# Attention on one core: the last ten pairs' queries and keys transposed by transfers inside SBUF

## The chip, the core and the metric

The kernel runs on one core of a Trainium2 chip. The metric is the device time of one execution in microseconds, lower is better; the inputs lie in HBM before, the output lies there after. The engines are PE (TensorE), DVE (VectorE), ACT (ScalarE), POOL (GpSimd) and SP (SyncE), which here only issues transfers. They run their own instruction streams in order and wait for each other through semaphores.

## What is computed

Softmax attention over 8 x 8 heads of 512 queries and 512 keys with 64 dimensions, in float32 at both ends:

```python
batch, heads, seq, dim = 8, 8, 512, 64
scale = 1.0 / np.sqrt(q.shape[-1])
scores = np.einsum('bhqd,bhkd->bhqk', q, k) * scale
attn = np.exp(scores - scores.max(axis=-1, keepdims=True))
attn = attn / attn.sum(axis=-1, keepdims=True)
return np.einsum('bhqk,bhkd->bhqd', attn, v)
```

## The kernel before

**Pairs and groups.** The 64 heads are taken two at a time: 32 pairs, numbered g from 0 to 31. Each head's 512 keys are four chunks c of 128. A block is one chunk of keys of one head against all 512 queries; a group is two blocks, in most pairs the same chunk of both heads. There are four groups a pair, 129 in all because the last is cut in two halves, and they are numbered m; group m belongs to pair m // 4 (the halves at the end aside).

**The way of one pair.** SP loads q, k and v of the pair, 256 KB each (L432; for v of pairs 20 to 24, `HALVED`, in two pieces, L430). POOL casts them to fp16: v into one of twelve tiles `vps` that hold a column of ones beside the 64 dimensions (L438), q and k into one tile `qkp` with both heads side by side (L448; five such tiles). PE transposes the eight 128x128 blocks of `qkp` into one PSUM tile (`transposes`, L472) and DVE copies that to SBUF as `tqk`, dimensions of both heads in the partitions (`copy`, L485; four such tiles). PE then makes the scores of a group: two matmuls of 64 x 512 that stand in the two halves of the array's rows (`scores`, L512), into one of three PSUM tiles `st`. ACT takes exp of the 128x1024 scores at once (L517) into one of 30 tiles `pt`. PE multiplies slices of 128 queries with the values (`values`, L619): a unit is one such slice of one head, four units a head, 65 columns each, the last the sum of the row. Seven units share a PSUM bank (two banks, which the transposes also use). DVE divides by the sum (`normalise`, L596 and L598) into a ring of 56 units in SBUF, and SP stores each head from there when its four units are done (L607, 128 KB).

**Groups on DVE.** For the groups in `ON_DVE` DVE replaces ACT's exp: `raise_` (L538) turns scores into the bits of a power of two and frees the `st` bank, and five passes (`pass_`, L552, L561, L571, L576 and L585) make from it two fp16 parts `pe` and `pd` whose sum is the exponential. The value matmuls of such a block run twice, once for each part.

**The order of the work.** Nothing is scheduled by a compiler: the order of each engine's stream comes from the class `Plan`, which steps through time with a duration for each kind of work and writes down what each engine takes next. `step_pe` prefers scores when a bank is free, then transposes of the next pair, then values. `step_dve` prefers copies that are needed soon, then raises, then normalises; passes go in where nothing else is due. `step_pool` and `step_dve` put out casts in the order of `self.due`, as soon as the load has landed and a `qkp` tile is free. A cast of pair g puts the load of pair g + 7 into SP's list (`emit`), since the float32 tile comes free with it (seven of each of q, k and v); `step_sp` works that list off in order, and normalises add stores to it. The first pair, its loads and the start are written out by hand (`first_pair`), and so are the last head's values (`last_values`, `finish`, L638 to L660). The plan only sets orders; on the chip each step still waits for its data.

Of the kernel before, what the change touches and what calls it, by code (L numbers as in the profile page):

```python
# [10 lines left out]
FP16 = mybir.dt.float16  # L11
U16 = mybir.dt.uint16
# [5 lines left out]
class Plan:  # L18
# [13 lines left out]
    STEP = 5  # L32
    CALM, KEEN = 9000, 4
    FIRST_UNIT = 4
    ON_DVE = (10, 16, 26, 34, 43, 52, 61, 68, 79, 82, 96, 105, 114)

    LATE_NORM, LATE_COPY, HURRY, SOON, BACKLOG = 1300, 1400, 900, 80, 1000
    SLACK, AHEAD = 0, 1
# [1 line left out]
    CAST, CAST_DONE, TO_POOL = 557, 130, 150  # L40
    FIRST_LAND, LOAD, STORE, LATENCY, ISSUE = 5200, 700, 350, 2300, 450
    RAW, QK16, NV = 7, 5, 12

    def __init__(self, groups, pairs, first):
        self.groups, self.pairs = groups, pairs
        self.pe, self.act, self.dve = 7000, self.FIRST_EXP, 6300
        self.pool, self.port, self.dma = 4600, 4600, self.FIRST_LAND
        self.m, self.tiled = first, True
        self.read = []
        self.exps = {}  # L50
        for m in range(first):
            self.act += self.EXP + self.EXP_FIXED
            self.exps[m] = self.act + self.EXP_DONE
            self.read.append(self.exps[m])
        self.tq = {0: 5800}
        self.transposed = {0: 5800}
        self.next_t = 1
        self.part_t = 0
        self.banks = [5100, 5800]
        self.todo = [(g, h) for g in range(pairs) for h in range(2)]  # L60
        self.last = self.todo.pop()
        self.last_part = 0
        self.head = None
        self.units = self.FIRST_UNIT
        self.member = {b: m for m, grp in enumerate(groups) for b in grp}
        self.ready = []
        self.passes = []
        self.passed = {}
        self.steps = []
        self.busy_dve = 0  # L70
        self.done_heads = 0

        late = {grp[0][0] for m, grp in enumerate(groups) if m in self.ON_DVE}
        due = []
        for g in range(pairs):
            scores = 5000 + 3380 * g
            if g:
                due += [(scores - 2300, g, "k"), (scores - 2290, g, "q")]
            due.append((scores + 4000 + (6000 if g in late else 0), g, "v"))
        self.due = sorted(due)  # L80
        self.uncast = list(self.due)
        self.casts = []
        self.landed, self.cast_done = {}, {}
        self.first_loads = [(g, n) for _, g, n in self.due if g < self.RAW]
        self.first_loads += [(self.RAW, "k"), (self.RAW, "q")]
        for x in self.first_loads:
            self.dma += self.LOAD
            self.landed[x] = self.dma
        self.loads = []
        self.sp = 1650 + 470 * len(self.first_loads)  # L90

    def note(self, t, *what):
# [2 lines left out]
    def emit(self, t, after):  # L95
        _, g, n = self.uncast.pop(0)
        shared = (g, n) == (1, "q")
        self.note(t, "cast", g, n, t > self.CALM)
        if not shared:
            self.casts.append((g, n, t if after is None else after + self.TO_POOL))  # L100
        if g + self.RAW < self.pairs:
            self.note(t, "load", g + self.RAW, n)
            self.loads.append(("load", g + self.RAW, n))
# [20 lines left out]
                self.cast_done[(g, n)] = t + self.CAST + self.CAST_DONE  # L124

    def step_sp(self, t):
        if not self.loads or self.sp > t:
            return
        what = self.loads[0]
        if what[0] == "load":  # L130
            _, g, n = what
            if g >= self.RAW and self.cast_done.get((g - self.RAW, n), 1e9) > t:
                return
            self.dma = max(self.dma, t + self.LATENCY - self.LOAD) + self.LOAD
            self.landed[(g, n)] = self.dma
        else:
            if what[1] > t:
                return
            self.dma = max(self.dma, t + self.LATENCY - self.STORE) + self.STORE
        self.loads.pop(0)  # L140
        self.sp = t + self.ISSUE
# [113 lines left out]
    def step_pe(self, t):  # L255
        if self.m == len(self.groups):
            self.values(t)
            return
        g = self.groups[self.m][0][0]
        backlog = self.act - t  # L260
        one, two = self.free() <= t, self.free(1) <= t
        if one and (two or backlog < self.HURRY or self.tiled):
            return self.scores(t)
        if not one and backlog < self.BACKLOG and self.free() < t + self.SOON:
            return
        if self.part_t:
            return self.transposes(t)
        if (
            self.next_t < self.pairs
            and self.next_t <= g + self.AHEAD  # L270
            and all(self.cast_done.get((self.next_t, n), 1e9) <= t for n in "kq")
            and self.bank(t) is not None
        ):
            return self.transposes(t)
        if not self.values(t) and one:
            self.scores(t)

    def step_dve(self, t):
# [8 lines left out]
        if now:  # L287
            g = self.groups[min(self.m + 1, len(self.groups) - 1)][0][0]
            job = min(now, key=lambda x: (x[1] != "copy" or x[2][0] > g, x[1] != "raise", x[0]))
            self.ready.remove(job)  # L290
            _, kind, what = job
# [8 lines left out]
            if kind == "norm":  # L300
                more = self.NORM_COLUMN * what[1]
                self.dve = t + self.NORM[0] + more
                self.banks[what[2]] = t + self.NORM[1] + more + self.TO_PE
                for _ in range((what[0] + what[1]) // 4 - what[0] // 4):
                    self.loads.append(("store", self.dve + 100))
            elif kind == "finish":
                self.dve = t + self.NORM[0] + 2 * self.NORM_COLUMN
            elif kind == "copy":
                held, done = self.COPY if what[0] != 1 else self.COPY_1
                self.dve = t + held  # L310
                self.banks[what[1]] = self.tq[what[0]] = t + done + self.TO_PE
            else:
                self.dve = t + self.RAISE[0]
                self.read[what[0]] = t + self.RAISE[1] + self.TO_PE
                self.passes += [(what[0], s) for s in range(len(self.PASSES))]
                self.passed = {(what[0], None): self.dve + self.PASS_DONE, **self.passed}
# [30 lines left out]
def kernel(  # L347
# [28 lines left out]
    cpool = ctx.enter_context(tc.tile_pool(name="const", bufs=1))  # L376
    lpool = ctx.enter_context(tc.tile_pool(name="load", bufs=7))
    qpool = ctx.enter_context(tc.tile_pool(name="qk16", bufs=5))
    tpool = ctx.enter_context(tc.tile_pool(name="tqk", bufs=4))
    ppool = ctx.enter_context(tc.tile_pool(name="pt", bufs=30))  # L380
    dpool = ctx.enter_context(tc.tile_pool(name="pd", bufs=4))
    wpool = ctx.enter_context(tc.tile_pool(name="work", bufs=2))
# [3 lines left out]

    NV = 12

    HALVED = range(20, 25)
    NU = 56  # L390
    ring = cpool.tile([P, NU, D], FP32, name="ring")
    vps = [cpool.tile([P, 2, NI, D + 1], FP16, name=f"vp{n}") for n in range(NV)]
# [14 lines left out]
    def source(src, g):  # L407
        b, h = g // ppb, 2 * (g % ppb)
        return src[b, h : h + 2].rearrange("h (p i) d -> p h i d", i=NI)
# [12 lines left out]
    def load(g, names):  # L422
        if g >= NP:
            return
        for name in names:
            src = {"q": q, "k": k, "v": v}[name]
            t = load_tile(g, name)
            if name == "v" and g in HALVED:
                for h in range(2):
                    nc.sync.dma_start(out=t[:, h], in_=source(src, g)[:, h])  # L430
                continue
            nc.sync.dma_start(out=t[:, :, :, :], in_=source(src, g))  # L432

    def cast(g, name):
# [29 lines left out]
    def transposes(g, n, bank):  # L464
        if n == 0:
            tqk[g] = tpool.tile([P, 2, S], FP16, tag="tqk", name=f"tqk_{g}")
        if n == 0 or g == 1:

            tps[g] = ps_x.tile([P, 2, NI, P], FP16, tag=f"x{bank ^ n}", name=f"tp_{g}_{n}")
        n = 1 - n  # L470
        for i in range(NI):
            nc.tensor.transpose(tps[g][:, n, i, :], qkp[g][:, n, i, :], ident)  # L472
        if g == 1 and n == 1:
            copy(g, n)

    def copy(g, n=0):
        if g == 1:
# [55 lines left out]

    def raise_(m):
        r = raised[m]
        r["u"] = wpool.tile([P, 2, S], U16, tag="u", name=f"u_{m}")
        dve(
            nc.vector.tensor_scalar(  # L538
                out=r["u"][:, :, :],
                in0=r["st"][:, :, :],  # L540
                scalar1=BITS,
                scalar2=BIAS,
                op0=AluOp.mult,
                op1=AluOp.add,
            )
        )
# [46 lines left out]
    def normalise(u, n):  # L593
# [8 lines left out]
                op=AluOp.mult,  # L602
            )
        )
        while heads and heads[0][2] + NI <= u + n:
            g, h, u0 = heads.pop(0)
            nc.sync.dma_start(  # L607
                out=source(out, g)[:, h], in_=ring[:, u0 % NU : u0 % NU + NI, :]
            )
# [152 lines left out]
    with tc.manual_schedule():  # L762
# [6 lines left out]
        for n in range(NV):  # L769
# [5 lines left out]
            "values": values,  # L775
            "load": load,
            "cast": cast_behind,
            "raise": raise_,
            "copy": lambda g, b: copy(g),
            "pass": pass_,  # L780
# [36 lines left out]
```

## Time and profile before

| | us |
|---|---|
| runs: 117.13, 117.09, 116.84; median | 117.09 |
| the profiled execution | 117.77 |
| its span, first to last instruction | 116.0 |
| DVE busy, with the four largest groups L598, L485, L538, L585 | 97.5: 22.6, 20.5, 15.8, 9.3 |
| POOL's casts of v, k, q | 20.2, 19.2, 18.4 |
| PE's scores, values from `pt`, transposes | 43.9, 45.2, 19.3 |
| SP's issues of 256 KB loads, from issue to landing | 5.0 to 5.3 |
| SP's issues of 128 KB stores, from issue to landing | 3.9 |

Busy times are of one execution with its own time, 117.77. An engine's mean time of one instruction counts from its start to its end; where the next one starts before that end, the two overlap, and the distance from start to start is what one of them really takes. HBM was read for 25.17 MB and written for 8.39 MB. The granted clock of TensorE was 0.999.

### The profile page before, as it was taken

Reading aid. Unit: us, or ns where it says so; the run is one execution under the profiler, and the core shown is the slowest. Engines: PE = TensorE matmul, PEld = TensorE weight load, DVE = VectorE, ACT = ScalarE, POOL = GpSimd, SP = SyncE. Lnnn points to the kernel's source line nnn. Section 1 sums busy time; section 2 is a strip of 40 time slices with the busy share of each in tenths; the row PEclk is TensorE's granted clock in tenths of the full one; section 3 lists DMA queues with packets and bytes.
Section 4 is the critical chain, followed back from the end, with each engine's and each line's share of the span. In section 5 each row is a group of like instructions: output and inputs, shape, how many; then the busy total and the mean of one; then the engine's idle time right before and its main releaser. Section 6 shows DMA issues by size and latency. Waiting matters only on the chain.

```text
span 116.0 us, 4294 instructions
## 1 busy us (share of the span) xinstructions
PE 105.4 (91%) x1663; PEld 69.5 (60%) x1663; DVE 97.5 (84%) x209; ACT 107.8 (93%) x120; POOL 57.6 (50%) x102
## 2 busy tenths in 40 slices
PE   7979988999999899999999999989999999999940
PEld 2545544665666557676655676558577667657630
DVE  1464599996999799999999999999999999996270
ACT  4499999999999999999999999999999999999930
POOL 2466836469464674753847568644634974000000
PEclk9999999999999999999999999999999999999999
DMA  3999999999999999999979999889998995821244
GB/s 95 323 328 374 384 378 383 384 380 374 381 333 330 309 362 324 305 318 356 369 248 291 319 317 295 266 264 338 346 310 267 361 309 171 266 94 50 91 138 138
DMA packets 35605, 33.84 MB, mean 292 GB/s; under 512 B 2688, under 2 KB 35584, under 8 KB 35584
## 3 DMA queue, kind: packets, MB, share of 16 engines
q1 hardware_dynamic: 35152, 33.24, 86.0%
q10 hardware_dynamic: 432, 0.33, 0.9%
q8 instruction: 13, 0.21, 0.8%
q14 instruction: 8, 0.07, 0.2%
HBM read 25.17 MB, written 8.39 MB: 289 GB/s over the span
## 4 chain that ended last, share of the span: by engine, by line
ACT 46%; PE 45%; issue 5%; DVE 2%; ACTq 0%
ACT pt L517 45%; PE st L512 17%; PE o L619 16%; PE tp L472 6%; PE st_0a L671 3%; ACT pt L721 1%; PE st L714 1%; PE tp_qb L709 0%; PE o_last L638 0%; DVE qt L751 0%; DVE ring L598 0%; PE tp_qa L709 0%; DVE obl L653 0%; PE st_0a L714 0%; DVE rc_last L652 0%
## 5 line engine op out<-in xcount | busy, mean ns | idle before, releaser
L517 ACT ACTIVATE pt<-st 128x1024 f16<-128x1024 f32 (+1 forms) x113 | 102.8, 1240 | 0.0
L512 PE MATMUL st<-tqk 64*128 64x512 f16 (+1 forms) x250 | 43.9, 380 | 4.0 <-ACT pt L517 2.7
L619 PE MATMUL o<-vp,pt 128*128 128x65 f16 x904 | 45.2, 195 | 0.5 <-POOL vp L438 0.2
L619 PEld LDWEIGHTS <-pt 128*128 128x128 f16 x904 | 38.5, 98 | 11.7 <-issue 8.7
L438 POOL CAST vp<-v 128x512 f16<-128x512 f32 x32 | 20.2, 631 | 13.4 <-DVE pd L585 5.0
L448 POOL CAST qkp<-q 128x512 f16<-128x512 f32 x30 | 18.4, 613 | 14.3 <-DVE pd L585 3.9
L448 POOL CAST qkp<-k 128x512 f16<-128x512 f32 x31 | 19.2, 619 | 9.2 <-PE st L512 2.2
L598 DVE TENSOR_TENSOR ring<-o,rc 128x448 f32<-128x448 f32 (+2 forms) x37 | 22.6, 612 | 1.3
L512 PEld LDWEIGHTS <-tqk 64*128 64x128 f16 x250 | 13.1, 93 | 16.7 <-issue 9.2
L485 DVE COPY tqk<-tp 128x1024 f16<-128x1024 f16 x30 | 20.5, 683 | 1.6 <-PE tp L472 1.4
L472 PE MATMUL tp<-ident,qkp 128*128 128x128 f16 x248 | 19.3, 220 | 0.4 <-DVE tqk L485 0.3
L472 PEld LDWEIGHTS <-qkp 128*128 128x128 f16 x248 | 14.1, 97 | 6.8 <-issue 3.9
L619 PE MATMUL o<-vp,pe 128*128 128x65 f16 x104 | 18.0, 195 | 0.2 <-DVE tqk L485 0.2
L619 PE MATMUL o<-vp,pd 128*128 128x65 f16 x104 | 17.9, 193 | 0.0
L538 DVE TENSOR_SCALAR u<-st 128x1024 uint16<-128x1024 f32 x13 | 15.8, 1217 | 1.6 <-PE st L512 1.5
L619 PEld LDWEIGHTS <-pe 128*128 128x128 f16 x104 | 10.2, 98 | 2.4 <-issue 2.4
L596 DVE RECIPROCAL rc<-o 128x7 f32<-128x7 f32 (+2 forms) x37 | 7.3, 196 | 5.0 <-PE o L619 4.6
L619 PEld LDWEIGHTS <-pd 128*128 128x128 f16 x104 | 10.2, 98 | 0.2 <-issue 0.2
L585 DVE TENSOR_TENSOR pd<-u,w 128x1024 f16<-128x1024 f16 x13 | 9.3, 714 | 0.2
L571 DVE TENSOR_TENSOR s<-m 128x1024 f16<-128x1024 f16 x13 | 8.8, 680 | 0.0
L552 DVE TENSOR_SCALAR m<-u 128x1024 uint16<-128x1024 uint16 x13 | 6.1, 470 | 0.1
L561 DVE TENSOR_SCALAR pe<-u 128x1024 uint16<-128x1024 uint16 x13 | 6.2, 476 | 0.0
(48 smaller groups left out, 32.3 us busy)
## 6 DMA issues: line engine op xcount, KB each, us to landing
out_dram<-ring SPq DMA_DIRECT2D x63, 128.0 KB, 3.9
k<-in_k_dram SPq DMA_DIRECT2D x31, 256.0 KB, 5.1
q<-in_q_dram SPq DMA_DIRECT2D x31, 256.0 KB, 5.3
v<-in_v_dram SPq DMA_DIRECT2D x27, 256.0 KB, 5.0
v<-in_v_dram SPq DMA_DIRECT2D x10, 128.0 KB, 4.0
k<-in_k_dram ACTq DMA_DIRECT2D x2, 128.0 KB, 2.9
q<-in_q_dram SPq DMA_DIRECT2D x2, 128.0 KB, 2.7
out_dram<-obl SPq DMA_DIRECT2D x1, 64.0 KB, 1.6
```

The source lines that it names most:

```text
L438: return nc.gpsimd.tensor_copy(out=vps[g % NV][:, :, :, 0:D], in_=raw[g]["v"][:, :, :, :])
L448: return nc.gpsimd.tensor_copy(out=dst, in_=src[:, :, :, :])
L472: nc.tensor.transpose(tps[g][:, n, i, :], qkp[g][:, n, i, :], ident)
L485: nc.vector.tensor_copy(out=tqk[g][:, :, :], in_=tps.pop(g).rearrange("p n i c -> p n (i c)"))
L512: nc.tensor.matmul(st[:, x, cols], kc, qc[:, cols], start=True, stop=True)
L517: nc.scalar.activation(out=pt[:, :, cols], in_=st[:, :, cols], func=EXP, scale=scale, bias=SHIFT)
L538: nc.vector.tensor_scalar(out=r["u"][:, :, :], in0=r["st"][:, :, :], scalar1=BITS, scalar2=BIAS, op0=AluOp.mult, op1=AluOp.add,)
L571: ins = nc.vector.tensor_tensor(out=r["s"][:, :, :], in0=mantissa, in1=mantissa, op=AluOp.mult)
L585: ins = nc.vector.tensor_tensor(out=r["rest"][:, :, :], in0=r["u"].bitcast(FP16)[:, :, :], in1=r["w"][:, :, :], op=AluOp.mult,)
L596: nc.vector.reciprocal(out=rc[:, 0:n], in_=o[:, x : x + n, D : D + 1])
L598: nc.vector.tensor_tensor(out=ring[:, u % NU : u % NU + n, :], in0=o[:, x : x + n, 0:D], in1=rc[:, 0:n].broadcast_to([P, n, D]), op=AluOp. ...
L619: nc.tensor.matmul(os[u // 7][:, u % 7, :], part[:, y * P : (y + 1) * P], vps[g % NV][:, h, c, :], start=(n == 0), stop=(n == len(parts) - 1),
```

## The change

Four things change.

- For the pairs from `TURNED` = 22 on, PE no longer transposes and DVE no longer copies. A transposing transfer that SP issues (`turn`) reads `qkp` and writes `tqk` in SBUF. The plan holds it back until the scores of pair g - 8 are made (eight `tqk` tiles now) and both casts are done, and counts 1500 ns of transfer time and 4000 ns to its landing. The casts of these pairs are due 9000 ns ahead of their scores in the plan, 2300 before.
- Two heads of a pair go out in one store where they follow each other and lie in the ring in one piece; heads at the end go out as before.
- The loads of v of pairs 20 to 24 are whole.
- Fourteen groups are on DVE, at other places; the tile `u` that `raise_` writes has four buffers, two before.

```diff
-    ON_DVE = (10, 16, 26, 34, 43, 52, 61, 68, 79, 82, 96, 105, 114)
+    ON_DVE = (8, 14, 23, 29, 41, 48, 58, 63, 69, 76, 87, 92, 107, 116)
...
+    TURNED, TQ = 22, 8
+    TURN, TURN_LATENCY, TURN_AHEAD = 1500, 4000, 9000
...
-                due += [(scores - 2300, g, "k"), (scores - 2290, g, "q")]
+                ahead = 2300 if g < self.TURNED else self.TURN_AHEAD
+                due += [(scores - ahead, g, "k"), (scores - ahead + 10, g, "q")]
...
+        if g >= self.TURNED and n == "q":
+            self.turns.append(g)
...
     def step_sp(self, t):
+        if self.turns:
+            g = self.turns[0]
+            if self.m > self.member[(g - self.TQ, 3, 1)]:
+                self.turns.pop(0)
+                self.note(t, "turn", g)
+                self.loads.append(("turn", g))
...
+        elif what[0] == "turn":
+            _, g = what
+            if max(self.cast_done.get((g, n), 1e9) for n in "kq") > t:
+                return
+            self.dma = max(self.dma, t + self.TURN_LATENCY - self.TURN) + self.TURN
+            self.tq[g] = self.transposed[g] = self.dma
...
-            self.next_t < self.pairs
+            self.next_t < self.TURNED
...
-                for _ in range((what[0] + what[1]) // 4 - what[0] // 4):
+                for _ in range((what[0] + what[1]) // 8 - what[0] // 8):
...
-    tpool = ctx.enter_context(tc.tile_pool(name="tqk", bufs=4))
+    tpool = ctx.enter_context(tc.tile_pool(name="tqk", bufs=Plan.TQ))
...
-    HALVED = range(20, 25)
...
-            if name == "v" and g in HALVED:
-                for h in range(2):
-                    nc.sync.dma_start(out=t[:, h], in_=source(src, g)[:, h])
-                continue
...
+    def turn(g):
+        tqk[g] = tpool.tile([P, 2, S], FP16, tag="tqk", name=f"tqk_{g}")
+        nc.sync.dma_start_transpose(
+            out=tqk[g].rearrange("p n (i c) -> p (n i) c", c=P),
+            in_=qkp[g].rearrange("p n i c -> p (n i c)"),
+        )
...
-        r["u"] = wpool.tile([P, 2, S], U16, tag="u", name=f"u_{m}")
+        r["u"] = wpool.tile([P, 2, S], U16, tag="u", name=f"u_{m}", bufs=4)
...
+        end = Plan.FIRST_UNIT + 4 * (2 * NP - 1)
         while heads and heads[0][2] + NI <= u + n:
-            g, h, u0 = heads.pop(0)
+            g, h, u0 = heads[0]
+            if h == 0 and u + n < end and u0 % NU + 2 * NI <= NU:
+                if len(heads) == 1:
+                    break
+                if heads[1] == (g, 1, u0 + NI):
+                    if u0 + 2 * NI > u + n:
+                        break
+                    del heads[:2]
+                    nc.sync.dma_start(
+                        out=source(out, g),
+                        in_=ring[:, u0 % NU : u0 % NU + 2 * NI, :].rearrange(
+                            "p (h i) d -> p h i d", h=2
+                        ),
+                    )
+                    continue
+            heads.pop(0)
             nc.sync.dma_start(
```

More of the change, by code (lines that the diff above doesn't have):

```diff
@@ L89, in __init__ @@
         self.loads = []
+        self.turns = []
+        self.stored = 0
         self.sp = 1650 + 470 * len(self.first_loads)
@@ L777 @@
             "cast": cast_behind,
+            "turn": turn,
             "raise": raise_,
```

## The prediction

> **What bounds the kernel now.** I read four views of the profile, in this order. First the page: busy shares, the chain and the costliest groups.
>
> ```profile
> span 116.0 us, 4294 instructions
> ...
> PE 105.4 (91%) x1663; PEld 69.5 (60%) x1663; DVE 97.5 (84%) x209; ACT 107.8 (93%) x120; POOL 57.6 (50%) x102
> ...
> q1 hardware_dynamic: 35152, 33.24, 86.0%
> ...
> ACT 46%; PE 45%; issue 5%; DVE 2%; ACTq 0%
> ...
> L517 ACT ACTIVATE pt<-st 128x1024 f16<-128x1024 f32 (+1 forms) x113 | 102.8, 1240 | 0.0
> ...
> L485 DVE COPY tqk<-tp 128x1024 f16<-128x1024 f16 x30 | 20.5, 683 | 1.6 <-PE tp L472 1.4
> L472 PE MATMUL tp<-ident,qkp 128*128 128x128 f16 x248 | 19.3, 220 | 0.4 <-DVE tqk L485 0.3
> ```
>
> By shares alone PE, DVE and ACT all look full, and the chain hands the time to ACT and PE about equally. The idle column decides: L517 never had its engine idle before it (0.0). Second, the timeline of ACT alone, which merges what runs without a gap:
>
> ```profile
> 7.53 1.02 ACT L721 ACTIVATE pt<-st 128x1024 f16<-128x1024 f32 x1 [0.28 <-PE st L714]
> 8.45 102.83 ACT L517 ACTIVATE pt<-st 128x1024 f16<-128x1024 f32 x113
> ```
>
> One unbroken stretch of 102.83 us: 111 full exponentials and two halves, so 102.83/112 = 0.918 us for each. The 1240 ns of the group row overlap; 0.918 is the price. The span is 8.45 us of start, this stretch to 111.28, and a tail of 4.7. PE's share of the chain is PE answering a bank that ACT has just released, inside ACT's queue. So only two things move the time: how many exponentials ACT makes, and whether one of them ever waits.
>
> Third, the same busy times by stage (columns: PE, PEld, DVE, ACT, POOL, clock, DMA share, GB/s):
>
> ```profile
> 60.00:70.00 10.00, 9.84 (x169) 6.73 (x169) 9.75 (x21) 10.00 (x12) 6.05 (x11) 1.00 0.94 299
> 70.00:80.00 10.00, 9.21 (x147) 5.88 (x147) 9.79 (x20) 10.00 (x12) 5.78 (x10) 1.00 0.89 282
> 80.00:90.00 10.00, 10.00 (x178) 6.99 (x175) 9.45 (x20) 10.00 (x13) 4.92 (x9) 1.00 0.97 313
> 90.00:100.00 10.00, 9.80 (x176) 6.80 (x173) 9.79 (x19) 10.00 (x12) 6.14 (x10) 1.00 0.83 278
> ```
>
> In the stretch where the new transfers run, 70 to 100 us, DMA already moves 282 to 313 GB/s. Fourth, DVE's timeline, where a start to the next start is what an operation really holds:
>
> ```profile
> 71.18 0.67 DVE L485 COPY tqk<-tp 128x1024 f16<-128x1024 f16 x1
> 71.78 1.21 DVE L538 TENSOR_SCALAR u<-st 128x1024 uint16<-128x1024 f32 x1
> 72.91 0.19 DVE L596 RECIPROCAL rc<-o 128x7 f32<-128x7 f32 x1
> 73.13 0.62 DVE L598 TENSOR_TENSOR ring<-o,rc 128x448 f32<-128x448 f32 x1
> 73.67 0.68 DVE L485 COPY tqk<-tp 128x1024 f16<-128x1024 f16 x1
> ```
>
> A copy holds 0.60, a raise 1.13, a normalise 0.76; the five passes, read the same way, 0.33, 0.33, 0.61, 0.46 and 0.61. A group on DVE holds 1.13 + 2.34 = 3.47 us.
>
> **The change, part by part.**
>
> *Fourteen groups on DVE for thirteen.* ACT makes 112 exponentials, not 113: one full one less, **-0.92 us**, on the path. DVE pays 3.47; PE pays 8 more value matmuls (104/13 = 8 a group), at some 0.034 apart 0.27 us, under ACT.
>
> *Ten pairs without transposes and copies.* PE loses 80 transposes; eight stand in the chain with 0.55, so 5.5 us. DVE loses 10 copies of 0.60, 6.0. Neither engine held ACT up in the stretch above, so this is worth nothing by itself; it pays for the 3.47 and 0.27. If the cover went (ACT no longer full), PE's 5.5 would count.
>
> *The new places.* Ten groups now stand at or before group 76, eight before. Scores of group 77 come when ACT has done 77-3-10 = 64 exponentials: 8.45 + 64 x 0.918 = 67.2 us. DVE, from its first copy at 8.1, has 59.1 us for 10 groups (34.7), 20 copies (12.0) and some 19 normalises (14.4): 61.1, 2.0 too much; with 8 groups it was 54.1 of 60.9. What is put off is passes (lowest in the planner's order; the u tiles go from two buffers to four, so several groups can wait). After that 44 us remain for 4 groups, 1 or 2 copies and 17 normalises, about 28. Bounds: 0 to +2.0 us; I take 0, since DVE was 98% busy from 60 to 80 before with ACT never idle. A late raise would hold one of the three score banks; the next-but-two scores wait behind it on PE, then ACT.
>
> *Ten transposing transfers on SP.* No row shows such a transfer. It moves 256 KB from SBUF to SBUF. Lower bound, as an ordinary load at the best rate in the page's slices (384 GB/s): 0.68 us of all 16 engines. Upper bound: a row of a transposed block is 128 fp16, 256 B, a quarter of the usual 1 KB packet; if each cost what a packet costs now (0.86 x 116.0 us x 16 / 35152 = 45 ns), 1024 of them take 2.9 us. From 70 to 100 us DMA moved (282 + 313 + 278) x 10 us = 8.73 MB, 22.7 us at 384 GB/s: 7.3 us are free. Ten turns need 6.8 at the lower bound, 29 at the upper. What doesn't fit eats lead. Pair 22's query cast (the 21st q row of L448) ended at 66.9; its first exponential, number 75 of L517's row, began near 8.45 + 75 x 0.918 = 77.3, now 0.9 sooner, and its scores must be begun some 0.9 (a slot of ACT, my estimate) before that: 75.5. So 8.6 us, less a landing of 5.1 to 5.3 like k and q loads: 3.4 of slack. The cast is due 6.7 us sooner (9000 for 2300), two pairs ahead in the order, and the five qkp buffers let it (its data landed long before): 10 us of slack. Cover: 7.3 + 10 = 17.3 us, or **1.73 us a turn**. Nearest row is the 256 KB load, so I take 0.68: cost 0 on the path; the upper bound costs 11.7 us.
>
> The Trainium skill, "DMA: Bandwidth & Descriptors", section Latency and other measured facts, gives a DMA transpose 261 GB/s where the middle dimension isn't contiguous and 350 to 400 where it is. By that page alone my estimate is 0.66 to 1.0 us a turn, inside the cover, and the sum would be the same with a smaller chance of late turns; no row of this trace shows such a transfer, so nothing here is built on it.
>
> *SP's queue.* A turn waits on SP for POOL's two casts and for PE's scores of pair g-8 (long done); behind it queue the loads and stores, and behind those POOL's casts and DVE's ring. SP already stands 8.2 us (17 times) on such casts without ACT noticing. Its issues fall: five v loads in one piece, -5; ring stores in twos where both heads lie in the 56-unit ring in one piece: pairs whose u0 % 56 is 52 (4 of 31) and the last stay single, so 63 becomes 36 if heads come in order; turns +10. Net -22 of about 0.43, so 9 us less on SP. A dispatch of a turn could take as long as the longest store's, 1.59 us: 10 x 1.2 more, near what was saved. Cost 0, bounds 0 and about +1 where a store blocks the ring. Same bytes, later by half a pair (1.7 us) against a ring seven pairs long: 0.
>
> *The tail.* After 111.28 come the last values, DVE's finish with a normalise between (0.55), and three stores; SP issued the last at 113.32, 0.8 us after its data (112.52), held up by a store that took 1.1 to issue. Fewer stores and a freer PE could take this out, or the normalise: -0.6 to +0.3. ACT's own last store at 112.96 stays, so I take -0.1.
>
> **Sum.** -0.92 + 0 + 0 + 0 - 0.1 = -1.0 us. The profiled execution took 117.77 (span 116.0 and 1.8 around it), giving 116.8; it was 0.68 above the median of the runs, 117.09, giving **116.1**, which I forecast.
>
> **Rivals.**
>
> *Turns land late* (slower). At 2.0 us a turn, ten need 20, 2.7 over the cover: PE stands at the first scores of a late pair, all PE work queues behind, ACT runs dry. 117.09 - 0.92 + 2.7 = 118.9. It decides from 1.73 us a turn. For it: DMA shares of 0.89 to 0.97, FIFO behind loads. Against: seven pairs of raw buffers, few loads left after 90 us. Chance 0.25.
>
> *VectorE becomes the bound before group 76* (no change). Half of the 2.0 lost as ACT waits after raises: 117.09 - 0.92 + 1.0 = 117.2. For: 61.1 in 59.1. Against: u's four buffers, DVE full before without harm. Chance 0.12.
>
> *Blocks one behind the other.* If each of a turn's eight 128x128 blocks took a latency of its own, as the smallest store here does (1.6 us), a turn would take 12.8 against 3.3 us a pair (102.83/31): 10 x 9.5 - 17 (the cover) = 78 us more, 117.09 - 0.92 + 78 = 194. Against: ordinary loads of 128 rows pay one latency. Chance 0.03. The Trainium skill, "VectorE: DVE Perf Modes", section The three transpose paths, gives 1309 ns for one 128x128 block by DMA against 390 on TensorE; eight in a row would be 10.5 us by that page. By that rule this change is a bad trade; no run here shows it yet.
>
> *Nothing else moves*: the forecast, 0.60.
>
> **Range and chances.** A measurement of this kernel can tell about 0.3% (0.35 us) from no change. Faster by more than that: 0.60, the forecast. Within it: 0.13 (DVE's bound, and mild lateness). Slower: 0.27 (late turns, one by one). The forecast's own range is 115.5 (the whole tail gain) to 116.6; the range, with the late turns up to 2.0 us, 115.5 to 118.9.
>
> **What would show it.** Right: L517 x112 in one stretch of about 101.9 us, idle 0.0; L485 x20; u x14; turns landing within 8 us of issue; ring stores near 36. Wrong: L517 with idle, released by PE whose scores waited for a DMA into tqk (late turns, after 75 us) or for u L538 (DVE, before 67 us); a DMA share at its ceiling from 70 to 100 us with POOL waiting for loads.

## The result: 121.46 us, 3.3% slower, and the profile after

The changed kernel takes 121.46 us (median of 120.67, 121.04, 121.87 and 123.31) against 117.11 before: ratio 1.0327, 95% interval 1.0266 to 1.0387. Executions fall into a faster and a slower state, and the ratio compares the faster ones (here without 123.31), so it is not the quotient of the two medians. The profiled execution took 121.87 with a span of 120.1, 4.1 more than before. On the page, the lines that answer to those shown of before:

```profile
span 120.1 us, 4117 instructions
...
PE 103.9 (87%) x1591; PEld 66.5 (55%) x1591; DVE 94.2 (78%) x205; ACT 107.6 (90%) x119; POOL 57.5 (48%) x102
...
PE 43%; ACT 22%; DVE 17%; DMA 10%; issue 5%; ACTq 0%
...
L538 ACT ACTIVATE pt<-st 128x1024 f16<-128x1024 f32 (+1 forms) x112 | 102.6, 1210 | 5.4 <-PE st L533 5.4
...
out_dram<-ring SPq DMA_DIRECT2D x25, 256.0 KB, 5.3
out_dram<-ring SPq DMA_DIRECT2D x13, 128.0 KB, 3.9
...
tqk<-qkp SPq DMA_TRANSPOSE x10, 4.8
```

The exponential is one less (x112), as meant; but ACT, which never stood, now stands 5.4 us, all of it released by PE's scores, and DMA has entered the chain with 10%. ACT's timeline says when:

```profile
8.43 71.60 ACT L538 ACTIVATE pt<-st 128x1024 f16<-128x1024 f32 x78
82.72 1.02 ACT L538 ACTIVATE pt<-st 128x1024 f16<-128x1024 f32 x1 [2.68 <-PE st L533]
83.92 1.02 ACT L538 ACTIVATE pt<-st 128x1024 f16<-128x1024 f32 x1 [0.18 <-PE st L533]
85.12 1.02 ACT L538 ACTIVATE pt<-st 128x1024 f16<-128x1024 f32 x1 [0.18 <-PE st L533]
87.47 1.02 ACT L538 ACTIVATE pt<-st 128x1024 f16<-128x1024 f32 x1 [1.32 <-PE st L533]
89.28 3.77 ACT L538 ACTIVATE pt<-st 128x1024 f16<-128x1024 f32 x4 [0.78 <-PE st L533]
93.35 23.09 ACT L538 ACTIVATE pt<-st 128x1024 f16<-128x1024 f32 x26 [0.30 <-PE st L533]
```

Up to 80.03 us the stretch is unbroken: nothing is lost in the two thirds with ten groups on DVE. Then six pauses, 5.44 us, and each restart costs 0.1 more (1.02 for an exponential begun on an idle engine, 0.92 in the stream). The sum: -0.92 for the exponential, +5.44 and +0.6 for the pauses, and a tail of 3.7 us after ACT's end at 116.44 where it was 4.7: +4.1, the whole difference of the spans.

PE's timeline names what PE itself waited for (the score rows among others):

```profile
81.29 0.39 PE L533 MATMUL st<-tqk 64*128 64x512 f16 x2 [2.58 <-DMA tqk<-qkp]
...
82.00 0.61 PE L533 MATMUL st<-tqk 64*128 64x512 f16 x2
...
86.97 0.39 PE L533 MATMUL st<-tqk 64*128 64x512 f16 x2 [1.95 <-DMA tqk<-qkp]
```

Two turns were late, those of pairs 23 and 24; the other pauses are what follows. In 82.00 two score matmuls take 0.61, not 0.39: the granted clock fell. By windows (columns as above: PE, PEld, DVE, ACT, POOL, clock, DMA share, GB/s):

```profile
80.00:84.00 4.00, 2.71 (x26) 1.43 (x27) 1.56 (x2) 1.14 (x3) 1.01 (x2) 0.70 1.12 355
84.00:88.00 4.00, 2.05 (x35) 1.23 (x33) 1.76 (x4) 2.50 (x3) 0.73 (x2) 0.88 1.29 207
88.00:92.00 4.00, 4.00 (x56) 2.16 (x52) 3.13 (x7) 3.22 (x4) 0.38 (x1) 0.57 1.09 324
```

A late turn was paid twice: once as the wait itself (ACT's pauses of 2.68 and 1.32 us, 4.0 of the 5.4), then as a clock of 0.57 to 0.88 at which PE is too slow to keep ACT fed (the other four pauses, 1.4 us, fall there or right behind; from 88 to 92 us PE is busy without a break and ACT still waits). The Trainium skill, "TensorE: Matmul & The Clock Gate", Part 1, says that the array runs at half rate after an idle window of some 3.4 us. The trace has the half rate, 0.50 from 82 to 84 and again from 89 to 91 us, but after pauses of 2.6 and 1.95 us, shorter than these 3.4. In experiment e9 below the clock is 0.66 from 96 to 100 us with no pause of PE above 0.52 us in the ten microseconds before. What sets it off is open here.

Why were they late? POOL's rows hold the query casts of pairs 23 and 24 (68.20 and 72.69), SP's the turns (the second number is the time that SP itself spent on the issue):

```profile
68.20 0.62 POOL L462 CAST qkp<-q 128x512 f16<-128x512 f32 x1 [0.60 <-DVE pd L606]
...
72.69 0.62 POOL L462 CAST qkp<-q 128x512 f16<-128x512 f32 x1 [1.17 <-DVE pd L606]
```

```profile
67.95 3.12 SPq L492 DMA_TRANSPOSE tqk<-qkp  x1
71.17 0.53 SPq L446 DMA_DIRECT2D v<-in_v_dram  x1
71.80 0.40 SPq L644 DMA_DIRECT2D out_dram<-ring  x1
72.30 0.38 SPq L446 DMA_DIRECT2D k<-in_k_dram  x1
72.77 0.50 SPq L446 DMA_DIRECT2D q<-in_q_dram  x1
73.37 0.42 SPq L446 DMA_DIRECT2D k<-in_k_dram  x1
73.88 0.42 SPq L446 DMA_DIRECT2D q<-in_q_dram  x1
74.39 0.42 SPq L636 DMA_DIRECT2D out_dram<-ring  x1
74.90 2.82 SPq L492 DMA_TRANSPOSE tqk<-qkp  x1
...
81.05 1.30 SPq L492 DMA_TRANSPOSE tqk<-qkp  x1
```

Pair 23's data were cast at 68.8, and SP issued the turn at 74.90: 6.1 us in which SP did nothing but work off its stream, the previous turn's 3.12 us first. Pair 24's: 73.3 and 81.05, 7.7 us. From the packets in the trace, pair 23's 1024 packets of 256 B ran from 78.4 to 80.7, and its scores began at 81.29. Cast to scores: 12.5 us, of which 6.1 passed before the issue, 3.5 from there to the first packet, 2.3 in the packets and 0.6 after them. PE ran out of other work at 78.71, 9.9 us after the cast. Even with a landing of 5.1 to 5.3 us, as the forecast had it, 6.1 us before the issue would have made the pair late.

### The profile page after: what moved, and what is told of

It reads as the page before. It is cut to its first block, busy times and chain, and to the rows that moved or that the text cites. A ratio compares the mean times of both kernels' runs of the same rounds, so it can differ in the third digit from the quotient of the medians.

```text
span 120.1 us, 4117 instructions
## 1 busy us (share of the span) xinstructions
PE 103.9 (87%) x1591; PEld 66.5 (55%) x1591; DVE 94.2 (78%) x205; ACT 107.6 (90%) x119; POOL 57.5 (48%) x102
## 4 chain that ended last, share of the span: by engine, by line
PE 43%; ACT 22%; DVE 17%; DMA 10%; issue 5%; ACTq 0%
ACT pt L538 22%; PE o L656 18%; PE st L533 17%; DMA tqk<-qkp 10%; DVE u L559 4%; PE tp L486 3%; DVE tqk L506 3%; PE st_0a L708 3%; DVE ring L619 2%; DVE s L592 2%; DVE m L573 1%; DVE pd L606 1%; DVE pe L582 1%; DVE w L597 1%; PE st L751 1%
## 5 line engine op out<-in xcount | busy, mean ns | idle before, releaser
L533 PE MATMUL st<-tqk 64*128 64x512 f16 (+1 forms) x250 | 45.5, 393 | 11.3 <-ACT pt L538 5.4
L452 POOL CAST vp<-v 128x512 f16<-128x512 f32 x32 | 19.4, 620 | 13.3 <-DVE s L592 4.9
L559 DVE TENSOR_SCALAR u<-st 128x1024 uint16<-128x1024 f32 x14 | 17.0, 1216 | 3.7 <-PE st L533 3.7
L656 PE MATMUL o<-vp,pe 128*128 128x65 f16 x112 | 19.6, 197 | 0.2
L656 PE MATMUL o<-vp,pd 128*128 128x65 f16 x112 | 19.5, 195 | 0.0
L486 PE MATMUL tp<-ident,qkp 128*128 128x128 f16 x168 | 14.0, 220 | 0.0
L506 DVE COPY tqk<-tp 128x1024 f16<-128x1024 f16 x20 | 13.6, 681 | 0.1
L656 PEld LDWEIGHTS <-pe 128*128 128x128 f16 x112 | 11.1, 99 | 3.2 <-issue 2.9
L486 PEld LDWEIGHTS <-qkp 128*128 128x128 f16 x168 | 9.6, 98 | 5.2 <-issue 2.9
L656 PEld LDWEIGHTS <-pd 128*128 128x128 f16 x112 | 11.2, 100 | 0.1
L597 DVE TENSOR_SCALAR w<-s 128x1024 f16<-128x1024 f16 x14 | 5.9, 421 | 0.2
```

The source lines that it names most:

```text
L452: return nc.gpsimd.tensor_copy(out=vps[g % NV][:, :, :, 0:D], in_=raw[g]["v"][:, :, :, :])
L506: nc.vector.tensor_copy(out=tqk[g][:, :, :], in_=tps.pop(g).rearrange("p n i c -> p n (i c)"))
L533: nc.tensor.matmul(st[:, x, cols], kc, qc[:, cols], start=True, stop=True)
L559: nc.vector.tensor_scalar(out=r["u"][:, :, :], in0=r["st"][:, :, :], scalar1=BITS, scalar2=BIAS, op0=AluOp.mult, op1=AluOp.add,)
L656: nc.tensor.matmul(os[u // 7][:, u % 7, :], part[:, y * P : (y + 1) * P], vps[g % NV][:, h, c, :], start=(n == 0), stop=(n == len(parts) - 1),
```

## The experiments

My theory A was that a turn is dear in a full queue; the rivals were SP's stream (B) and the new places (C). Each experiment was timed beside the kernel before on its own chip; ratios are against that.

**e1: ordinary transfers in place of the turns.**

```diff
-        nc.sync.dma_start_transpose(
-            out=tqk[g].rearrange("p n (i c) -> p (n i) c", c=P),
-            in_=qkp[g].rearrange("p n i c -> p (n i c)"),
-        )
+        nc.sync.dma_start(
+            out=tqk[g][:, :, :], in_=qkp[g].rearrange("p n i c -> p n (i c)")
+        )
```

> The changed kernel with each of the ten transposing transfers replaced by an ordinary transfer of the same 256 KB from qkp to tqk, at the same place of SP's order (the late pairs' scores are then made from untransposed data). Theory A, the transposing transfer itself is dear (it holds SP 1.2 to 3.1 us and stops the 16 DMA engines until the last of them has come to it): dispatch falls to about 0.5 us, no late pair, ACT without idle from its first exponential on, 115.5 to 117. Theory B, any transfer at these places of SP's stream is late, because SP was 3 us behind its plan already and the loads stand ahead of it: landings stay 6 us behind the casts, ACT idles 3 to 5 us, 119 to 121. Theory C, the new places of the groups on DVE: unchanged, 121.

Measured: four runs of 116.79, 119.11, 119.17 and 120.36, ratio 1.014 (1.005 to 1.022). The profiled one is that of 116.79: dispatch 0.47 us, landing 3.6 (median), ACT idle 0.29 us in the late stretch. Pair 23's transfer was still issued 3.6 us behind its cast (69.5, 73.06), pair 24's 4.2. So the transposing kind of transfer costs a good part, some 1.9 of the 3.3%, and SP's stream is behind even without it. That this is what made the other three runs longer is argued: they left no trace. It doesn't decide between A and B; with ACT fed and the new places kept, C falls.

**e2: no turns at all** (`TURNED, TQ = 32, 8`).

> The changed kernel with TURNED = 32: all pairs transposed on PE and copied by DVE, with the fourteen places, whole v loads and stores in twos kept; the plan is made anew for it. Theory A: ACT idle near 0, its stretch 101.9 us; PE and DVE have more left at the end, so the tail is 0 to 1 us longer: 116.5 to 118. Theory C (the places overload DVE before group 76): ACT idles 1 us or more behind raises before 67 us, 118 or more.

Measured: 119.18, ratio 1.012 (1.004 to 1.020), above the 116.5 to 118 of theory A. ACT's timeline:

```profile
7.74 101.92 ACT L538 ACTIVATE pt<-st 128x1024 f16<-128x1024 f32 x112
```

101.92 us without a gap: the fourteen places starve ACT nowhere. But the span is 117.0, so the tail is 7.3 us after ACT's end at 109.66, where before it was 4.7: after ACT's end DVE works for another 3.6 us (two full normalises, one of four units and the two of the last head), before for 1.6. Without the relief of the turns the fourteenth group is paid back at the end, and more.

**e3: the thirteen old places, turns kept.**

```diff
-    ON_DVE = (8, 14, 23, 29, 41, 48, 58, 63, 69, 76, 87, 92, 107, 116)
+    ON_DVE = (10, 16, 26, 34, 43, 52, 61, 68, 79, 82, 96, 105, 114)
```

> The changed kernel with the thirteen old places, turns and stores in twos kept. Theory A: the turns are as dear as before, so pairs 23 and 24 are late again, a little less since ACT is up to 1.8 us later there: ACT idles 2 to 5 us, 119 to 122. Theory C: back to 117.

Measured: 124.11, ratio 1.052 (1.044 to 1.060), ACT idle 6.2 us after 80 us, PE waiting 5.2 us three times for turns. That is above the 119 to 122 expected. The loss stays without the new places, so it is the turns that lose the time. The longest of the three waits, 3.9 us, is for pair 26's turn; and with the old places ACT makes one exponential more, 0.9 us.

**e4: stores in twos and whole v loads alone** (the old places, `TURNED, TQ = 32, 8`).

> Only the stores in twos and the whole v loads: TURNED = 32 and the thirteen old places. Theory A: nothing on the path, 116.8 to 117.4, the same as before. A rival, that stores in twos or whole v loads hold up the ring or POOL: slower by 0.5 us or more.

Measured: 117.36, ratio 0.9973 (0.9938 to 1.0008): no change that can be told. The trace shows a side effect that matters below. From 30 to 60 us:

```profile
30.00:60.00 30.00, 28.45 (x455) 18.95 (x451) 28.58 (x56) 30.00 (x34) 17.20 (x29) 1.00 1.09 379
```

379 GB/s, where the same window has 333 before the change, and 330 in e12, whose stores go one head at a time. In the stream of instructions that the kernel is built to, each transfer on SP waits for the landing of the one eight places ahead, whatever its size. The changed kernel's trace agrees: its twelve issues from 60.6 to 68 us each start 0.02 to 0.18 us after that landing. Larger transfers carry more through eight places. So with stores in twos the loads run further ahead and DMA is full until 80 us: 29.2 MB moved by then, 26.1 before.

**e5 and e6: turns for the last four and six pairs**, with the plan told what a turn took here. e6:

```diff
-    ON_DVE = (8, 14, 23, 29, 41, 48, 58, 63, 69, 76, 87, 92, 107, 116)
+    ON_DVE = (8, 14, 23, 29, 41, 50, 58, 63, 69, 76, 89, 95, 107, 116)
...
-    TURNED, TQ = 22, 8
-    TURN, TURN_LATENCY, TURN_AHEAD = 1500, 4000, 9000
+    TURNED, TQ = 26, 8
+    TURN, TURN_LATENCY, TURN_AHEAD = 2800, 4000, 9000
+    TURN_ISSUE = 1500
...
-        self.sp = t + self.ISSUE
+        self.sp = t + (self.TURN_ISSUE if what[0] == "turn" else self.ISSUE)
```

e5 has the same with `TURNED, TQ = 28, 8` and the places (8, 12, 22, 29, 37, 45, 55, 61, 71, 77, 89, 98, 108, 116).

> Turns for the last four pairs alone (TURNED = 28), the plan told what a turn cost in the changed kernel (2.8 us of transfer time, 1.5 us of SP), fourteen groups on DVE at places that suit that plan. Theory A (a turn is dear only while loads fill the 16 DMA engines and SP is behind): these four run when most loads are in, none is late, ACT idle under 0.3 us, its stretch 101.9 us: 115.8 to 116.8, 0.5 to 1% faster than before. Rival, a turn is dear wherever it stands or the plan's model is off: one of the four late, 117.5 or more.

> The same with six pairs (TURNED = 26) and the fourteen places of the changed kernel but for three moved by 2 or 3. Theory A: pairs 26 and 27 fall into the end of the loads (casts near 80 us, turns 4 to 8 us behind); idle 0 to 1.5 us, 116 to 117.7. Rival (only the number of pairs counts, 6/10 of the loss): 119 to 120.

Measured: e5 116.32, ratio 0.990 (0.984 to 0.995); **e6 115.27, ratio 0.981 (0.975 to 0.986)**, faster than both kernels and than I expected. In e6 all 112 exponentials run without a gap from 7.62 us on, 102.09 in all. Its first turns on SP:

```profile
77.67 2.32 SPq L493 DMA_TRANSPOSE tqk<-qkp  x1
80.41 0.38 SPq L637 DMA_DIRECT2D out_dram<-ring  x1
80.91 1.76 SPq L493 DMA_TRANSPOSE tqk<-qkp  x1
```

The turns start when the loads of k and q are over; between the first two SP has one issue, between the second and the third (84.94) four, not seven, and each turn's last packet ends 4.8 to 7.2 us ahead of its scores (1.5 for pair 22 of the changed kernel, and too late for 23). The gain is the one exponential (102.09 us for 102.83) and a shorter tail (3.5 us against 4.7). The two spans differ by 0.8 us more, because this execution's stretch began at 7.62 and not at 8.45; in the traces here that start lies anywhere from 7.6 to 10.0 us, so I count it as chance.

**e7: ten spare turns that nobody waits for**, added to e4 behind the query casts:

```diff
+        if g >= 22 and n == "q":
+            self.note(t, "spare", g)
...
+    def spare(g):
+        t = tpool.tile([P, 2, S], FP16, tag="spare", name=f"spare_{g}", bufs=2)
+        nc.sync.dma_start_transpose(
+            out=t.rearrange("p n (i c) -> p (n i) c", c=P),
+            in_=qkp[g].rearrange("p n i c -> p (n i c)"),
+        )
```

> Stores in twos alone (experiment e4, thirteen old places, all pairs transposed on PE) with ten spare transposing transfers of pairs 22 to 31 added, each behind its query cast, into a tile that nothing reads. Theory A: each still takes 2 to 4 us of the engines when loads are queued and 1.2 us or more of SP, but nobody waits for its data; the loads it delays have leads of several us: ACT idle 0 to 1.5 us, 117 to 119. Rival D (the standstill of the engines alone starves the kernel through late loads): ACT idle 3 us or more, 120 to 122.

Measured: 118.23, ratio 1.005 (1.001 to 1.009), against 0.997 for e4; ACT idle 0.22 us. As traffic ten turns cost less than 1%. The other loss of the changed kernel is waiting for their data: rival D falls.

**e8: e1 with two transfers of 512 B ahead of each.**

```diff
+        for n in range(2):
+            nc.sync.dma_start(out=nothing[:, n], in_=ident[:, 0:2])
         nc.sync.dma_start(
             out=tqk[g][:, :, :], in_=qkp[g].rearrange("p n i c -> p n (i c)")
         )
```

> Experiment e1 (ordinary transfers in place of the turns) with two tiny transfers (512 B each) issued on SP just ahead of each, so that SP is held about 1.4 us a pair as by a turn in a quiet queue, without the engines standing still. If SP's hold is what makes the pairs late: issues 6 to 8 us behind the casts as in the changed kernel, ACT idle 3 to 5 us, 119.5 to 121.5. If it is the engines' standstill: as e1, its runs from 116.8 to 119.2, idle under 1.5 us in the profile.

Measured: 128.14, ratio 1.090 (1.085 to 1.096), 9 us over e1 and beyond both outcomes. Pair 23's transfer was issued at 79.63, 11 us behind its cast: SP's stream, with no turn in the kernel, is enough to bring pairs late, so theory A as I held it is not the whole matter. But the tiny transfers are not all that differs from e1. From 10 to 60 us DMA moved 356 GB/s here and 375 in e1, both at a full share (1.09 and 1.08), and SP came to pair 22's place at 71.71 (67.81 in e1) before it had issued any tiny transfer. That is 3.9 of the 6.6 us by which pair 23's transfer is later than in e1; the tiny ones took 1.3 us a pair. Why the loads ran slower was not tried, so e8 gives no price for a tiny transfer. It does show that one holds its place as long as a large one: the first, 512 B, landed 5.4 us after its issue.

**e9: the changed kernel with 14 loads fewer.** The loads of v of pairs 18 to 31 are left out, their values made with pair 16's v.

```diff
+            if name == "v" and g >= 18:
+                raw.setdefault(g, {})["v"] = raw[16]["v"]
+                continue
             src = {"q": q, "k": k, "v": v}[name]
```

> The changed kernel, all ten turns at the same places of SP's order, without the loads of v of pairs 18 to 31 (their values are made with pair 16's v): 14 transfers of 256 KB and their issues fewer, most of them in the stretch before and among the turns. Theory A (turns come late because SP's stream and the 16 engines are full of loads): issues come within 2 us of the casts, a turn takes 1.2 us of the engines, no late pair, ACT idle under 0.5 us, 115.5 to 116.8. Rival, a turn is dear and late by itself: idle 3 us or more, 119 or more.

Measured: 116.2, ratio 0.989 (0.980 to 0.998): ten turns, and ACT runs without a pause from 9.85 to 100.03 us. The profiled execution is the longest of the four, 117.59; it has one late pause, 0.88 us at 100 us (0.5 was expected at most), at the end of the low clock named above and not behind a turn. Pair 23's turn is issued at 71.43, 2.1 us behind its cast, pair 24's at 76.33 (2.5; PE still waited 0.57 us for it). The turns are not faster (the packets of the first four run for 2.3 to 3.0 us, in the changed kernel for 1.5 to 3.8); they are only issued sooner, and then ten of them are harmless. The edit takes places out of SP's stream and bytes off the engines at once, so it doesn't tell which of the two made the issues late; e12 sets them against each other.

**e10: six pairs with the changed kernel's places and the plan's old price** (`TURNED, TQ = 26, 8` alone), and **e11: eight pairs** (`TURNED, TQ = 24, 8`, else as e6).

> Six pairs (TURNED = 26) with the changed kernel's own fourteen places and its plan's old price of a turn (1500 ns, SP 450): tells what of experiment e6 came from the number of pairs and what from the plan's price and the three moved groups. If the number of pairs: within 0.5 us of e6, 115 to 116. If the price: one of the first two turned pairs late, 116.5 to 118.

> Eight pairs (TURNED = 24) with e6's places and prices: pairs 24 and 25 turn while loads still fill the engines. Theory A: their turns 6 to 8 us behind the casts, one or both late by 0 to 2 us: 115.5 to 118, slower than e6. Rival (only the price in the plan mattered): as e6, 115.3.

Measured: e10 116.05, ratio 0.987 (0.982 to 0.991); e11 118.47, ratio 0.997 (0.989 to 1.006), its eight runs from 116.26 to 121.73. So the number of pairs makes most of e6's gain; price and places make some 0.7 us, and the two intervals overlap. With eight the time can't be told from that of the kernel before (117.87 beside it). In the profiled execution (118.6) the second turn, pair 25's, kept PE waiting for 2.5 us, pair 29's for 1.1.

**e12: the changed kernel without stores in twos and whole v loads.**

```diff
-                for _ in range((what[0] + what[1]) // 8 - what[0] // 8):
+                for _ in range((what[0] + what[1]) // 4 - what[0] // 4):
...
-            if h == 0 and u + n < end and u0 % NU + 2 * NI <= NU:
+            if False and h == 0 and u + n < end and u0 % NU + 2 * NI <= NU:
...
+            if name == "v" and g in range(20, 25):
+                for h in range(2):
+                    nc.sync.dma_start(out=t[:, h], in_=source(src, g)[:, h])
+                continue
             nc.sync.dma_start(out=t[:, :, :, :], in_=source(src, g))
```

> The changed kernel with stores of one head each and the v loads of pairs 20 to 24 in two pieces, as before the change; turns and fourteen places kept. In the changed kernel, as in e4, DMA ran at 377 to 379 GB/s from 30 to 60 us, 333 before: larger transfers let SP's stream carry more, so the loads run further ahead and fill the engines just where the first turns come. If that fullness is what delays the first turns: DMA falls back to about 335 GB/s there, pair 23's turn is issued less than 6 us behind its cast, ACT idle under 3 us, 117 to 119.5. If SP's number of issues is what delays them: 33 more issues of 0.43 us and more, the turns come later still, idle 5 us or more, 121 to 125.

Measured: 127.51, ratio 1.081 (1.073 to 1.090). It is slower even than the 121 to 125 expected of SP's issues. DMA is less full (330 GB/s, as said above; from 65 to 70 us 283, where the changed kernel has 364), and yet the first turn is issued at 73.74 (67.95 with stores in twos), the second at 82.16 (74.90), and ACT's longest pause is twice as long:

```profile
81.88 1.02 ACT L542 ACTIVATE pt<-st 128x1024 f16<-128x1024 f32 x1 [5.18 <-PE st L537]
```

The two outcomes were set against each other, and the number of issues won over the fullness of the engines.

## Why the prediction was wrong

The forecast was 116.1 and the range ended at 118.9; 121.46 lies outside. By its own steps:

- **ACT bounds the kernel, one exponential less is -0.92 us: right.** e2 shows 101.92 us for 112, e6 102.09.
- **The new places cost 0: right.** No pause before 80 us here, none at all in e2's 101.92 us.
- **PE's and DVE's relief is worth nothing by itself: wrong at the end of the kernel.** e2 has the fourteen groups without it, and its tail is 7.3 us. The table of stages that I read ended at 100 us, where ACT still covers everything; behind ACT's last exponential nothing covers.
- **SP's queue, "Cost 0, bounds 0 and about +1": the step that failed.** I counted how many issues fall (63 stores to 36; they became 38) and took the average, where the question was what stands in SP's stream between a cast and its turn. For pair 23 that was the rest of a turn and seven issues, for pair 24 a whole turn and nine; a turn held SP for 2.8 to 3.1 us there and an issue came every 0.54, not 0.43. And I let the lead begin at the cast ("So 8.6 us, less a landing of 5.1 to 5.3"): the issues came 6.1 and 7.7 us after the casts for the two pairs that were late, so of 8.6 us only 2.5 and 0.9 were left for a landing. The time goes with that delay: for pair 23 it is 2.1 us in e9, 6.1 here, 11 in e8 and 13.3 in e12, at 116.2, 121.46, 128.1 and 127.5 us, so only roughly. None of the three moves the delay alone (fewer bytes in e9, slower loads in e8, smaller transfers in e12); the delay is what they have in common.
- **The cast two pairs sooner, 6.7 us: did not come.** The query casts of pairs 22 to 25 ended at 64.6, 68.8, 73.3 and 76.9; before, at 66.9, 70.4, 73.2 and 77.3. So they came 2.3, 1.6, -0.1 and 0.4 us sooner. In the plan's order only pair 22's casts moved, ahead of pair 21's: one pair, not two. What holds the casts was not tried apart.
- **0.68 us a turn: mis-sized.** In a quiet queue the 1024 packets run for 1.0 us (pairs 26 and 27, 91.1 to 92.1 and 93.4 to 94.4); among loads for 1.5 to 3.8 us (pairs 22 to 25). The Trainium skill, "DMA: Bandwidth & Descriptors", section Latency and other measured facts, has 261 GB/s for a transpose whose middle dimension isn't contiguous; 256 KB in 1.0 us, 262 GB/s, agrees, in a quiet queue only.
- **7.3 us of DMA free between 70 and 100: read from the wrong kernel.** The same change fills DMA at 375 GB/s until its first turns; the free time lies behind 80 us, where e6 has nearly all of its turns. (The rows that I quoted for 70 to 100 us also run from 278, not 282.)
- **The tail, -0.1: was -1.05.** ACT's pauses gave PE and DVE time to catch up, but e6, whose ACT never pauses, has a tail of 3.5 us too; and e2, with the fourteen places and without the relief, has 7.3; so it is the relief, which I had set at nothing.

The profile before had a warning for the step that failed. In the view of SP's waits, from which I took the 8.2 us on casts, stand also (us in total, times, longest):

```profile
SPq L432 <- DMA q<-in_q_dram: 4.0, 10, 0.9
SPq L432 <- DMA k<-in_k_dram: 3.1, 11, 0.4
```

SP's loads already stood on the landings of earlier transfers, so a place in its stream cost more than the 0.43 us of an issue.

The rival "turns land late" is what happened, by the wait that I named for it; I gave it 0.25 and a price of 2.7 us, and the measured one is 6.0. Its price took a turn's size for the cause. The two waits alone made 4.0 us, and it lacked the second payment, the clock after PE's pause.

What stays open: how the turn's own share divides between its issue on SP (1.24 to 3.12 us) and the engines' standstill described below, since e1 removes both at once; and what makes an issue of a turn take 1.24 us one time and 3.12 another.

## What to carry to other kernels

A transfer's lead starts when its queue reaches it, not when its data are ready: lay the issuing engine's timeline beside the producer's and count what stands between them. In a stream where each transfer waits for an earlier landing, an issue costs its place whatever its size, so small stores that nobody waits for can delay a transpose that somebody does (e12). When a trick costs more than planned, first try it on fewer pieces where the queue is emptier: ten pairs lost 3.3%, the last six won 1.9%.

## What the runs showed that I had not expected

**A transposing transfer gathers all the DMA engines.** Its packets in the changed kernel's trace, for pair 22's turn, in flight at each moment:

```
us      1 KB packets   256 B packets held open
70.0        16                 0
71.0         8                13
72.0         2                19
73.0         2                21
73.25        0                22
74.0        16                 0
```

As the ordinary packets run out, packets of the turn are opened and stay open; 21 of them, opened between 70.6 and 72.7 us, all end between 73.27 and 73.31, and more than half of the 1024 end between there and 74.0. Little else moves meanwhile (GB/s is the last column):

```profile
71.00:72.00 1.00, 1.00 (x26) 0.77 (x26) 0.97 (x3) 1.00 (x2) 0.52 (x1) 1.00 1.84 140
72.00:73.00 1.00, 1.00 (x25) 0.74 (x21) 0.97 (x3) 1.00 (x2) 0.32 (x1) 1.00 0.28 40
```

The reading, argued from this picture alone, is that engines which have come to the turn wait there for those still busy with loads. In a quiet queue (pairs 26 and 27) there is no such standstill: no packet takes longer than 25 ns.

**Stores in twos and whole loads raised the transfer rate** from 333 to 379 GB/s over 30 us with the same bytes to move (e4), and going back to single ones cost 6 us beside the turns (e12 over the changed kernel): places in SP's stream, and not only bytes, were scarce.
